# A new order of work in the mixer, and the final norm's third root placed sooner, in a hybrid attention and pooling layer

## The chip, the cores and the metric

The kernel runs on one core of one Trainium2 chip. A core has a matrix engine, TensorE (PE in the profile; PEld is its loading of stationary operands), and three others: VectorE (DVE), ScalarE (ACT) and GpSimd (POOL). SyncE (SP) only starts transfers. Each engine works through its own list in order and waits on semaphores for the others. Matmuls write to PSUM, eight banks of 128 x 512 float32; the other data lie in SBUF. The metric is the time of one execution in microseconds of device time, as the median of several.

## What is computed

One layer in float32: a half-weighted SwiGLU feed-forward block, a mixer, a second feed-forward block, and a norm of the rows. The sequence has 512 positions of 1024 channels.

```python
x = x + 0.5 * swiglu_ffn(rmsnorm(x, ffn1_norm), w_gate1, w_up1, w_down1)
x = x + hybrid_mixer(rmsnorm(x, mix_norm), w_in, ...)
x = x + 0.5 * swiglu_ffn(rmsnorm(x, ffn2_norm), w_gate2, w_up2, w_down2)
x = rmsnorm(x, final_norm)

def hybrid_mixer(h, ...):
    proj = h @ w_in                        # q, k, v, u, 512 channels each
    a = chunked_attention(q, k, v, ...)    # 8 heads of 64; q, k normed; bias; softmax
    p = multiscale_pool(u, ...)            # trailing means over 2, 4, 8, 16 minus the frame, then a 128 x 128 map
    return jnp.concatenate([a, p], axis=-1) @ w_out
```

A chunk of 64 positions attends to itself and the eight before it. With 512 positions that is every earlier chunk, so the scores are causal by blocks.

## The kernel before

All products are made from float32 values split in two parts, high (`whi`, `hhi`) and low (`wlo`, `hlo`): three matmuls (`mm3`, L176 to L178) stand for one product, a "unit" in what follows. ACT makes the high part and DVE subtracts it for the low part. The two feed-forward blocks use a product scheme with fewer multiplications, run by `ffn_up` and `Down`; the change does not touch their loops.

The mixer (from L894 on) works on tiles of 128 positions (t from 0 to 3). Its parts are Python generators:

- `project_qk` makes q and k of four heads (a half, 32 units, four PSUM banks of the tag `mm`); ACT empties each bank, scaled by the norm, into a row tile. `qk_norm` squares the rows (ACT), sums them per head (DVE, L1091), takes the reciprocal root on DVE (`rsqrt`), scales the four row tiles (DVE, L1122), has PE transpose them (L1130), and splits the result.
- `project_v` and `project_u` make v (32 units) and the four groups of pooled channels (8 units each). `pool` empties u on DVE (L1302), adds shifted copies on GpSimd (L1310: one addition for window 2, four for window 16), and finishes on DVE (L1317 to L1323); `pool_map` multiplies by the group's matrix.
- `scores` multiplies q by k for a pair of heads (L1201). Head dimension 64 fills half of PE's rows, so the two heads' matmuls go to the two halves by turns. Tile t has (t + 1) x 128 columns. `softmax` adds the bias, takes the row's minimum of the negated scores (DVE, L1170), exponentiates (ACT, L1176) and scales (ACT, L1182).
- `head` transposes the probabilities on PE (L1243) in three groups, splits them (L1222, L1225), multiplies by v (L1255) and splits the result (L1265 to L1270). Scores, transposes, head products and pool maps all take banks of the tag `a`, of which there are four.
- `project_out` makes the output projection (64 units) as its operands become ready, and `add` adds it to the residual and starts the next norm.

What stands where on PE, DVE, ACT and GpSimd is set by a planner, `run_parts` (L917). It keeps a model clock per engine; a part that has work gives its cost to `on`, and a part is taken when the time that it yields has come on PE's clock. Among parts that are ready the lowest rank is taken (`RANK_QK`, `RANK_HEAD`, `RANK_POOL`, `RANK_SCORES`, plus an entry of `RANKS`). `until` also holds a part back while an engine's model clock is over `SLACK` ahead of PE's. `products` is the background stream; `ORDER` sets it: before, first half of q and k, one group of u, second half, v, then three groups of u, then the output. The order thus planned is what the engines execute; the semaphores only say when.

```python
ORDER = (0, "u", 1, "v", "u", "u", "u")
RANK_QK, RANK_HEAD, RANK_POOL, RANK_SCORES = 1.5, 1.0, 1.035, 0.95
SLACK = 2.5
ACT_FIX, DVE_FIX, QK_NORM, NORM = 0.18, 0.08, 2.73, 3.5
```

The final norm is spread over the last product of the second feed-forward block. Rows are finished in tiles of 128; the third and fourth (t = 2, 3) come last. The last PSUM accumulations are p7: the third row's left half in one bank, the fourth row's in two banks of 256 columns. `residual` (L1475) adds a bank to the row, `settle` squares it with a sum over the row (ACT, L1488; DVE, L1483, for the very last part), `finish` takes the root on ACT (L1512), refines its reciprocal on DVE (`rsqrt_of`, L263 to L266), multiplies and stores (L1520, L1530).

Of the kernel before, what the change touches and what calls it, by code (L numbers as in the profile page):

```python
# [8 lines left out]
F32 = mybir.dt.float32  # L9
# [35 lines left out]
ORDER = (0, "u", 1, "v", "u", "u", "u")  # L45
RANK_QK, RANK_HEAD, RANK_POOL, RANK_SCORES = 1.5, 1.0, 1.035, 0.95
HOP = 0.1
SLACK = 2.5
ACT_FIX, DVE_FIX, QK_NORM, NORM = 0.18, 0.08, 2.73, 3.5
AHEAD, NORM_AT, FILL_AT, QK_ROOT = 2, 3, 7, ()  # L50
RANKS = {}

@with_exitstack
def layer(
# [202 lines left out]
    def rsqrt_of(v, root, out):  # L257

        n = v.shape[-1]
        y, a, b = (  # L260
            small.tile([P, n], F32, tag=f"rs{n}", name=name("rs"), bufs=3) for _ in range(3)
        )
        nc.vector.reciprocal(y, root)  # L263
        nc.vector.tensor_tensor(a, y, y, op=ALU.mult)
        nc.vector.scalar_tensor_tensor(b, a, -0.5, v, op0=ALU.mult, op1=ALU.mult)
        nc.vector.scalar_tensor_tensor(out, b, 1.5, y, op0=ALU.add, op1=ALU.mult)  # L266
# [627 lines left out]
    with tc.tile_pool(name="mix", bufs=1, reuse_waits="tile") as mpool:  # L894
# [51 lines left out]
        def t_mm3(n):  # L946
            return 3 * max(n / 2400, 0.107)
# [91 lines left out]

        qT, kT, aT, pT_out = [None] * 4, [None] * 4, [None] * 4, [None] * 4  # L1040
# [39 lines left out]
        def qk_norm(half, raw):  # L1080
# [38 lines left out]
            for t in range(NT):  # L1119
                yield from until(0.0, "dve")  # L1120
                q3 = raw[t][0].rearrange("p (h c) -> p h c", c=HD)
                nc.vector.tensor_tensor(  # L1122
                    q3, q3, rs[:, t, :].unsqueeze(2).to_broadcast([P, 8, HD]), op=ALU.mult
                )
                f = on("dve", t_dve(S))
            for j in (0, 2, 1, 3):
                yield from until(f)
                tp = yield from take("a")
                for t in range(NT):
                    nc.tensor.transpose(  # L1130
                        tp[:, t * P : (t + 1) * P], raw[t][0][:, j * P : (j + 1) * P], ident
                    )
                g = on("pe", 0.44)
                yield from until(g, "act", "dve")
                hi, lo = mtile(), mtile()
                split(tp, hi, lo, qk_sb[:, j // 2 : j // 2 + 1])
                g = on("dve", t_dve(S), on("act", t_act(S)))
                room["a"].append(g)
                (qT, kT)[j // 2][2 * half + j % 2] = (hi, lo), g
# [22 lines left out]
        def softmax(h, t, sc, f):  # L1162
# [8 lines left out]
                p, sc[:, :n], bias[h][0][:, S - n :], -1.0, BIG, op0=ALU.add, op1=ALU.min, accum_out=nm  # L1171
            )
            f = on("dve", t_dve(n))
            room["a"].append(f)
# [10 lines left out]
        def scores(pair):  # L1185
# [7 lines left out]
            for t in range(NT - 1, -1, -1):  # L1193
                n = (t + 1) * P
                sc = []
                for h in heads:
                    sc.append((yield from take("a")))
                for a, b in ((0, 0), (0, 1), (1, 0)):
                    for i in range(2):
                        rows = slice(i * HD, (i + 1) * HD)  # L1200
                        nc.tensor.matmul(  # L1201
                            sc[i][:, :n], qT[pair][0][a][rows, t * P : (t + 1) * P],
                            kT[pair][0][b][rows, :n], start=a + b == 0, stop=a == 1,
                        )
                f = on("pe", 2 * t_mm3(n))
                for i, h in enumerate(heads):
                    start(softmax(h, t, sc[i], f), RANK_HEAD + 0.01 * h, ("softmax", h))
                yield 0.0
            scored.update(heads)

        def head(h):
# [19 lines left out]
            for group in ((1, 3), (0,), (2,)):  # L1231
# [13 lines left out]
                start(evacuate(group, at, n, tp, on("pe", n / P * 0.11)), RANK_HEAD + 0.01 * h, ("turn", h))  # L1245
# [13 lines left out]
            f = on("pe", sum(t_mm3(n * P) for n in range(1, 5)) * 2 / 3)  # L1259
# [34 lines left out]
        def pool():  # L1294
            for g in (3, 2, 1, 0):
# [9 lines left out]
                s, step = u, 1  # L1305
                while step < win:
# [146 lines left out]
    with tc.tile_pool(name="act2", bufs=1, reuse_waits="tile") as apool:  # L1453
# [40 lines left out]
        def column(what):  # L1494
            return small.tile([P, 1], F32, tag="rc", name=name(what), bufs=6)
# [12 lines left out]
        def finish(t, v, part):  # L1508

            root, r = column("root"), column("r")  # L1510
            last = ssq[:, t, part : part + 1]
            nc.scalar.activation(root, last, AF.Sqrt, scale=1.0 / D, bias=v)  # L1512
            total = column("v")
            nc.vector.scalar_tensor_tensor(total, last, 1.0 / D, v, op0=ALU.mult, op1=ALU.add)
            rsqrt_of(total, root, r)
# [70 lines left out]
        with tc.manual_schedule(engines={E.PE, E.DVE, E.Activation}):  # L1586
            for tt in range(2):
                t = 2 + tt
                for i, at in enumerate(p7[tt]):
                    for g, a, w in late:  # L1590
                        down2.mms([[at]] * 2, g, a, w, (tt,), further=True)
                    residual(0, t, *at, scale=-0.5)
                    if i == 0 and tt:
                        settle(0, t, 0, *at[1:])
                        finish(t - 1, mean(t - 1, [1]), 0)
                        v = mean(t, [1, 0])
                    else:
                        settle(0, t, 2 * i, *at[1:])
            finish(t, v, 2)
# [81 lines left out]
```

## Time and profile before

| what | us |
|---|---|
| median of 3 runs (863.21 to 864.59) | 863.34 |
| the profiled execution | 864.34 |
| its span, from the first to the last instruction | 862.5 |
| busy in the span: PE | 846.9 |
| busy in the span: DVE | 715.1 |
| busy in the span: ACT | 501.4 |
| busy in the span: GpSimd | 120.5 |
| the mixer, some 354 to 527 us of the span | 173 |

In the profile L12 is line 12 of the kernel. A group of instructions is told as line, engine, operation, output<-inputs by the program's tile names, shape and count. A busy time counts an instruction from its start to its end; matmuls overlap, so that one of 512 columns lasts about 0.39 us while the next starts some 0.23 us after it. Where rows of a timeline have brackets, these hold the engine's idle time just before and who ended it. In a list of waits the columns are the total, how often, and the longest.

### The profile page before, as it was taken

How to read it: one execution, taken by the hardware profiler on the slowest of the kernel's cores; microseconds unless marked ns; L12 is line 12 of the kernel's file. 1: busy time of each engine (PE TensorE's matmuls, PEld its weight loads, DVE VectorE, ACT ScalarE, POOL GpSimd, SP SyncE). 2: the span in 40 equal slices, each digit the busy share in tenths (PEclk: the TensorE clock that was granted, in tenths of full speed). 3: DMA queues.
4: the chain of work that ended last, by engine and by line, in shares of the span. 5: the costliest groups of instructions: out<-in, count | busy, mean ns of one | idle time of the engine just before them, and what ended most of it. 6: DMA issues, size and time to landing. Idle time of an engine off the chain costs nothing.

```text
span 862.5 us, 14105 instructions
## 1 busy us (share of the span) xinstructions
PE 846.9 (98%) x5288; PEld 753.1 (87%) x5288; DVE 715.1 (83%) x1122; ACT 501.4 (58%) x859; POOL 120.5 (14%) x196
## 2 busy tenths in 40 slices
PE   9999999999999999989999999999999999999996
PEld 7889999999988888867878788889999999978885
DVE  7998889898897769685878667989988898787896
ACT  7445555555676556548647756355555555666573
POOL 0124322222000000120011000112121111122000
PEclk9999999999999999999999999999999999999999
DMA  8199998877576763322212026248778778899832
GB/s 291 55 279 258 302 267 200 201 214 167 150 235 205 251 210 135 102 86 84 75 56 92 25 73 230 89 146 228 216 227 208 191 200 222 251 317 351 256 107 98
DMA packets 72244, 158.50 MB, mean 184 GB/s; under 512 B 6112, under 2 KB 29168, under 8 KB 71792
## 3 DMA queue, kind: packets, MB, share of 16 engines
q1 hardware_dynamic: 49088, 110.93, 37.2%
q0 software_dynamic: 22656, 46.14, 24.8%
q8 instruction: 41, 0.67, 0.3%
q10 hardware_dynamic: 432, 0.54, 0.2%
q14 instruction: 27, 0.22, 0.1%
HBM read 153.38 MB, written 50.34 MB: 236 GB/s over the span
## 4 chain that ended last, share of the span: by engine, by line
PE 86%; DMA 6%; DVE 4%; ACT 2%; issue 1%; SPq 1%; ACTq 0%; DVEq 0%
PE mm L176 20%; PE mm L178 20%; PE mm L177 20%; PE a L176 7%; PE a L178 7%; PE a L177 7%; DMA raw<-in_wA_dram 4%; DMA raw<-in_wB_dram 1%; PE a L1201 1%; DVE wlo L478 1%; PE a L1255 1%; PE a L1243 1%; ACT whi L473 1%; DVE t L1122 1%; ACT prob L1182 1%
## 5 line engine op out<-in xcount | busy, mean ns | idle before, releaser
L131 ACT CAST whi<-raw 128x1024 fp32r<-128x1024 f32 (+2 forms) x115 | 107.4, 945 | 58.8 <-PE mm L177 17.4
L132 DVE TENSOR_TENSOR wlo<-raw,whi 128x1024 fp32r<-128x1024 f32 (+2 forms) x115 | 124.9, 1094 | 17.6 <-ACT whi L131 17.0
L176 PE MATMUL mm<-ha,whi 128*128 128x256 f32 x408 | 115.1, 282 | 0.0
L178 PE MATMUL mm<-ha,wlo 128*128 128x256 f32 x408 | 115.1, 282 | 0.0
L177 PE MATMUL mm<-ha,whi 128*128 128x256 f32 x408 | 114.6, 281 | 0.0
L569 ACT ACTIVATE t<-mm 128x256 f32<-128x256 f32 x102 | 39.1, 384 | 118.3 <-PE mm L178 117.5
L478 DVE TENSOR_TENSOR wlo<-wsum,whi 128x1024 fp32r<-128x1024 f32 x68 | 82.9, 1219 | 13.3 <-ACT whi L473 13.2
L177 PEld LDWEIGHTS mm<-ha,whi 128*128 128x128 f32 x408 | 77.4, 190 | 0.1
L176 PEld LDWEIGHTS mm<-ha,whi 128*128 128x128 f32 x408 | 77.2, 189 | 0.1
L178 PEld LDWEIGHTS mm<-ha,wlo 128*128 128x128 f32 x408 | 77.1, 189 | 0.0
L176 PE MATMUL mm<-hhi,whi 128*128 128x512 f32 x192 | 76.0, 398 | 0.3 <-ACT whi L131 0.3
L178 PE MATMUL mm<-hhi,wlo 128*128 128x512 f32 x192 | 75.0, 392 | 0.0
L177 PE MATMUL mm<-hlo,whi 128*128 128x512 f32 x192 | 74.8, 391 | 0.0
L706 POOL DMA_DIRECT2D wsum<-in_wB_dram x72 | 71.4, 1170 | 11.6 <-issue 8.2
L704 POOL COPY mark<-t 128x1 f32<-128x1 f32 x40 | 17.0, 425 | 379.3 <-DVE t L614 225.0
L473 ACT CAST whi<-wsum 128x1024 fp32r<-128x1024 f32 x68 | 67.8, 1045 | 3.1 <-PE mm L177 2.9
L177 PE MATMUL mm<-wlo,ah 128*128 128x512 f32 x176 | 68.8, 391 | 0.0
L178 PE MATMUL mm<-whi,ah 128*128 128x512 f32 x176 | 68.8, 391 | 0.0
L176 PE MATMUL mm<-whi,ah 128*128 128x512 f32 x176 | 68.6, 391 | 0.0
L478 DVE TENSOR_TENSOR wlo<-raw,whi 128x512 fp32r<-128x512 f32 x68 | 62.5, 951 | 5.5 <-ACT whi L473 3.4
L473 ACT CAST whi<-raw 128x512 fp32r<-128x512 f32 x68 | 56.3, 828 | 12.1 <-DMA raw<-in_wA_dram 12.0
L132 DVE TENSOR_TENSOR ah<-acts,ah 128x512 fp32r<-128x512 f32 (+1 forms) x72 | 45.7, 640 | 17.3 <-ACT ah L131 17.0
(224 smaller groups left out, 2380.1 us busy)
## 6 DMA issues: line engine op xcount, KB each, us to landing
raw<-in_wA_dram SPq DMA_DIRECT2D x87, 512.0 KB, 5.8
wsum<-in_wB_dram POOLq DMA_DIRECT2D x60, 512.0 KB, 7.5
raw<-wsum SPq DMA_DIRECT2D x40, 512.0 KB, 4.3
raw<-in_wB_dram SPq DMA_DIRECT2D x30, 512.0 KB, 4.8
wsum<-wsum POOLq DMA_DIRECT2D x20, 512.0 KB, 5.8
x<-in_xT_dram SPq DMA_DIRECT2D x16, 256.0 KB, 5.6
raw<-in_wQK_dram SPq DMA_DIRECT2D x8, 512.0 KB, 3.6
raw<-in_wO_dram SPq DMA_DIRECT2D x8, 512.0 KB, 3.4
```

Source lines behind the costliest of these rows:

```text
L131: nc.scalar.copy(hi, src)
L132: nc.vector.tensor_tensor(lo, src, hi.bitcast(F32), op=ALU.subtract)
L176: nc.tensor.matmul(acc, a[0], b[0], start=start, stop=False, **more)
L177: nc.tensor.matmul(acc, a[0], b[1], start=False, stop=False, **more)
L178: nc.tensor.matmul(acc, a[1], b[0], start=False, stop=stop, **more)
L473: nc.scalar.copy(hi, src)
L478: nc.vector.tensor_tensor(lo, src, hi.bitcast(F32), op=ALU.subtract)
L569: nc.scalar.activation(dst, src, AF.Copy, scale=scale)
L704: nc.gpsimd.tensor_copy(mark, after[:, 0:1])
L706: nc.gpsimd.dma_start(self.rows(i, g), self.rows(self.terms[i][at], g), **(dict(accum_op=ALU.add) if at else {}),)
L1122: nc.vector.tensor_tensor(q3, q3, rs[:, t, :].unsqueeze(2).to_broadcast([P, 8, HD]), op=ALU.mult)
L1182: nc.scalar.activation(p, p, AF.Copy, scale=rt)
```

## The change

The mixer's order is planned anew, and three pieces of code move.

- `ORDER` puts the second half of q and k directly behind the first; the first group of u follows it. Ranks, slack and the planner's costs are other numbers, `RANKS` gets entries, and the model cost of a unit is now 3 x (n / 2400 + 0.02) us.
- `scores` no longer goes tile by tile from 3 to 0, each in banks of its own. `GROUPS` says for each pair which tiles go together: a group is a list of bank sets, a bank set a list of tiles that lie side by side in one bank per head. For the first pair tiles 2 and 0 share a bank, then tiles 3 and 1 follow each other in two bank sets; for the other pairs tiles 1 and 0 share a bank. `softmax` gets its part of the bank, and the bank counts as free after its last tile.
- `pool` holds the planning of GpSimd's additions for a group back until a number of row tiles (`POOL_AFTER`) have been scaled by `qk_norm`.
- In the final norm the third row's root (`root_of`) is put on ACT right behind its square, ahead of the fourth row's square, and the reciprocal is refined in four DVE instructions in a row behind a halving, where it had five with the sum; the small tiles of `rsqrt_of` and of the columns get more buffers.

```diff
-ORDER = (0, "u", 1, "v", "u", "u", "u")
-RANK_QK, RANK_HEAD, RANK_POOL, RANK_SCORES = 1.5, 1.0, 1.035, 0.95
+ORDER = (0, 1, "u", "v", "u", "u", "u")
+RANK_QK, RANK_HEAD, RANK_POOL, RANK_SCORES = 1.66, 1.47, 0.935, 0.92
 HOP = 0.1
-SLACK = 2.5
+SLACK = 1.8
+POOL_AFTER = (8, 8, 7, 6)
+GROUPS = (
+    (((2, 0),), ((3,), (1,))),
+    (((1, 0),), ((2,),), ((3,),)),
+    (((3,),), ((2,),), ((1, 0),)),
+    (((1, 0),), ((2,),), ((3,),)),
+)
+STEP, SWITCH, TURN = 0.02, 0.32, 0.11
...
@@ scores @@
-            for t in range(NT - 1, -1, -1):
-                n = (t + 1) * P
+            for group in GROUPS[pair]:
                 sc = []
-                for h in heads:
-                    sc.append((yield from take("a")))
-                for a, b in ((0, 0), (0, 1), (1, 0)):
...
+                for _ in group:
+                    sc.append([])
+                    for h in heads:
+                        sc[-1].append((yield from take("a")))
+                on("pe", 2 * SWITCH)
+                for ts, banks in zip(group, sc):
+                    at = 0
+                    for t in ts:
+                        n = (t + 1) * P
+                        for a, b in ((0, 0), (0, 1), (1, 0)):
+                            for i in range(2):
+                                rows = slice(i * HD, (i + 1) * HD)
+                                nc.tensor.matmul(
+                                    banks[i][:, at : at + n],
+                                    qT[pair][0][a][rows, t * P : (t + 1) * P],
+                                    kT[pair][0][b][rows, :n], start=a + b == 0, stop=a == 1,
+                                    skip_group_check=True,
+                                )
+                        at += n
+                        f = on("pe", t_mm3(n))
...
@@ pool @@
+                while n_scaled[0] < POOL_AFTER[g]:
+                    yield None
                 while step < win:
...
@@ final norm @@
-        def finish(t, v, part):
+        def root_of(t, v, part):
+            root = column("root")
+            nc.scalar.activation(root, ssq[:, t, part : part + 1], AF.Sqrt, scale=1.0 / D, bias=v)
+            return root
+
+        def finish(t, v, part, root=None):
...
-            nc.scalar.activation(root, last, AF.Sqrt, scale=1.0 / D, bias=v)
-            total = column("v")
-            nc.vector.scalar_tensor_tensor(total, last, 1.0 / D, v, op0=ALU.mult, op1=ALU.add)
-            rsqrt_of(total, root, r)
+            nc.vector.tensor_scalar(half, v, -0.5, None, op0=ALU.mult)
+            nc.vector.scalar_tensor_tensor(
+                total, last, -0.5 / D, half, op0=ALU.mult, op1=ALU.add
+            )
+            nc.vector.reciprocal(y, root)
+            nc.vector.scalar_tensor_tensor(a, y, y, total, op0=ALU.mult, op1=ALU.mult)
+            nc.vector.scalar_tensor_tensor(r, a, 1.5, y, op0=ALU.add, op1=ALU.mult)
...
+            settle(0, first, 0, *p7[0][0][1:])
+            root = root_of(first, before, 0)
+            for i, at in enumerate(p7[1]):
+                for g, a, w in late:
+                    down2.mms([[at]] * 2, g, a, w, (1,), further=True)
+                residual(0, last, *at, scale=-0.5)
+                settle(0, last, 2 * i, *at[1:])
+                if i == 0:
+                    finish(first, before, 0, root)
+                    v = mean(last, [1, 0])
+            finish(last, v, 2)
```

On PE, DVE and ACT only the mixer and the final norm differ between the two programs; SP issues two loads and the bias rows in another order, and on GpSimd the bias tiles of heads 4 and 5 come ahead of the first pooled group's additions instead of behind.

72 lines of the change are left out of this document (37 added, 35 removed).

## Prediction

> **What bounds the kernel now.** I read the chain of waits first, by engine:
>
> ```profile
> PE 86%; DMA 6%; DVE 4%; ACT 2%; issue 1%; SPq 1%; ACTq 0%; DVEq 0%
> ```
>
> The end hangs on TensorE (PE) nearly all the way, so a new order can win only three things: time in which PE stands still, time it pays for changing between kinds of matmul, and the tail, where no matmul is left. Next I cut the span into stretches. The columns are the stretch, its length, then the busy time of PE, PE's weight loads, VectorE (DVE), ScalarE (ACT) and GpSimd (POOL), the granted clock and the DMA's share:
>
> ```profile
> 354.00:527.00 173.00, 168.64 (x864) 134.54 (x863) 122.31 (x281) 107.32 (x220) 16.55 (x26) 1.00 0.24 83
> 372.00:380.00 8.00, 5.39 (x24) 3.81 (x23) 7.14 (x9) 0.37 (x1) 5.40 (x4) 1.00 0.18 66
> 484.00:492.00 8.00, 6.38 (x42) 5.45 (x41) 3.95 (x9) 5.39 (x14) 0.00 (x0) 1.00 0.01 2
> 841.00:862.50 21.50, 13.77 (x89) 12.36 (x87) 13.86 (x42) 6.94 (x17) 0.00 (x0) 0.91 0.25 98
> ```
>
> The first row is the mixer: PE idles 173.00 - 168.64 = 4.36 us there. The next two rows hold nearly all of it: 8.00 - 5.39 = 2.61 us and 8.00 - 6.38 = 1.62 us. The last row is the final norm; there PE is without work for 21.50 - 13.77 = 7.7 us. The list of PE's waits (350 to 530 us; total, times, longest) names who was late:
>
> ```profile
> PE a L1130 <- DVE t L1122: 1.4, 2, 1.1
> PE mm L176 <- DVE u L1302: 1.2, 1, 1.2
> PE a L1243 <- DVE m L1270: 1.1, 1, 1.1
> PE a L1243 <- ACT prob L1182: 0.5, 1, 0.5
> ```
>
> The first two lie in 372:380: the transposes of q and k wait for DVE's scaled rows, and a projection waits for a PSUM bank that DVE empties into u. The other two lie in 484:492, at the transposes of heads 6 and 7. DVE's and GpSimd's timelines (start, length, line) tell why the scaled rows are late:
>
> ```profile
> 374.13 5.08 DVE L1122 TENSOR_TENSOR t<-t,z 128x512 f32<-128x512 f32 x4
> ...
> 415.75 2.49 DVE L1122 TENSOR_TENSOR t<-t,z 128x512 f32<-128x512 f32 x4
> ```
>
> ```profile
> 375.81 4.54 POOL L1310 TENSOR_TENSOR us<-us 128x525 f32<-128x525 f32 x3
> ```
>
> The same four scalings take 5.08 us while GpSimd sums and 2.49 us, with the other half of q and k, while it does not. So GpSimd's sums cost DVE 2.59 us there.
>
> **Term 1, the early stall.** Both halves of q and k are now projected before u. On DVE, in the mixer behind the first half's reciprocal root, stood before (t are the rows of q and k, z the root, u the pooled channels):
>
> ```order
> L995 TENSOR_TENSOR wlo_4302<-raw_4194,whi_4301 128x1024
> L1302 TENSOR_TENSOR u_4320<-mm_4242,rb_4202 128x512
> L1122 TENSOR_TENSOR t_4210<-t_4210,z_4294 128x512
> L1122 TENSOR_TENSOR t_4218<-t_4218,z_4294 128x512
> L1122 TENSOR_TENSOR t_4228<-t_4228,z_4294 128x512
> L1122 TENSOR_TENSOR t_4246<-t_4246,z_4294 128x512
> ```
>
> and stands now, at the same place:
>
> ```order
> L1009 TENSOR_TENSOR wlo_4306<-raw_4199,whi_4305 128x1024
> L1137 TENSOR_TENSOR t_4210<-t_4210,z_4289 128x512
> L1137 TENSOR_TENSOR t_4220<-t_4220,z_4289 128x512
> L1137 TENSOR_TENSOR t_4231<-t_4231,z_4289 128x512
> L1137 TENSOR_TENSOR t_4249<-t_4249,z_4289 128x512
> L1009 TENSOR_TENSOR wlo_4340<-raw_4243,whi_4339 128x1024
> ```
>
> The emptying of u, which released GpSimd's sums, is gone from in front of the scalings. Without the sums, rows that begin at 374.13 end at 374.13 + 2.49 = 376.6 and not at 374.13 + 5.08 = 379.2: 2.59 us sooner, and the missing u is worth about another 0.6. PE also has 17 units of three matmuls between the first half's projection and its transposes, where it had 15 (8 of u, 7 of the second half): two units more, 1.4 us at 0.23 us a matmul (the starts of two rows in the next term). That is some 4.6 us of room against 2.61 us of idle time: the whole 2.61 us goes, with 2 us to spare; if the cover failed, 2.61 us is what comes back.
>
> **Term 2, fewer changes to scores.** The scores use half of PE's rows, and each stretch of them pays at both edges. PE's timeline has two separate stretches (tiles of 256 and 128 columns) and the same two joined:
>
> ```profile
> 409.81 0.40 PE L178 MATMUL mm<-whi,hlo 128*128 128x512 f32 x1
> 410.13 0.62 PE L1201 MATMUL a<-m,m 64*128 64x256 f32 x6
> ...
> 412.26 0.55 PE L1201 MATMUL a<-m,m 64*128 64x128 f32 x6
> ...
> 413.08 0.39 PE L177 MATMUL mm<-wlo,hhi 128*128 128x512 f32 x1
> ```
>
> ```profile
> 475.08 0.39 PE L177 MATMUL mm<-m,whi 128*128 128x512 f32 x1
> 475.31 0.40 PE L178 MATMUL mm<-m,wlo 128*128 128x512 f32 x1
> 475.63 0.90 PE L1201 MATMUL a<-m,m 64*128 64x256 f32 x12
> ...
> 476.80 0.40 PE L177 MATMUL mm<-m,whi 128*128 128x512 f32 x1
> ```
>
> Ordinary matmuls start 0.23 us apart (475.31 - 475.08). From 409.81 to 413.08 are 3.27 us with eight of them (1.84 us): the two stretches cost 1.43 us. Joined: 476.80 - 475.31 = 1.49 us less two ordinary ones is 1.03 us. A join saves 0.40 us. On PE, in the scores of heads 0 and 1 (L1201 before, L1224 now; a are the score banks), stood before between two tiles a unit of projection:
>
> ```order
> L1201 MATMUL a_4425<-m_4374,m_4355 128x384
> L1201 MATMUL a_4439<-m_4374,m_4355 128x384
> L176 MATMUL mm_4316<-whi_4236,hhi_3926 128x512
> L177 MATMUL mm_4316<-wlo_4237,hhi_3926 128x512
> L178 MATMUL mm_4316<-whi_4236,hlo_3927 128x512
> L1201 MATMUL a_4446<-m_4374,m_4354 128x256
> L1201 MATMUL a_4451<-m_4374,m_4354 128x256
> ```
>
> and now one tile follows another, into the same two banks:
>
> ```order
> L1224 MATMUL a_4389<-m_4368,m_4357 128x384
> L1224 MATMUL a_4390<-m_4368,m_4357 128x384
> L1224 MATMUL a_4389<-m_4368,m_4356 128x128
> L1224 MATMUL a_4390<-m_4368,m_4356 128x128
> L1224 MATMUL a_4389<-m_4369,m_4356 128x128
> L1224 MATMUL a_4390<-m_4369,m_4356 128x128
> L1224 MATMUL a_4389<-m_4368,m_4357 128x128
> L1224 MATMUL a_4390<-m_4368,m_4357 128x128
> L190 MATMUL mm_4245<-whi_4239,hhi_3982 128x512
> ```
>
> Over the four pairs the order of before has 14 unbroken stretches (4, 4, 4 and 2), the new one 8 (two a pair, since where the plan has three groups two follow each other). Six joins at 0.40 us: -2.4 us. No row shows two tiles of scores in one bank. A join into a shared bank streams the same columns with the same weights, so it may save the whole 0.40; at worst it saves nothing. I take 0.40, the measured row being the nearest.
>
> **Term 3, the late stall.** On PE, at the first transposes of head 7 (prob), stood before, right behind the last two of head 6:
>
> ```order
> L1243 MATMUL a_5647<-ident,prob_5481 128x128
> L1243 MATMUL a_5647<-ident,prob_5468 128x128
> L1243 MATMUL a_5663<-ident,prob_5533 128x128
> L1243 MATMUL a_5663<-ident,prob_5486 128x128
> L1243 MATMUL a_5663<-ident,prob_5473 128x128 x2
> ```
>
> and now, with five units of the output projection, fifteen rows, between head 6 and these; the last two units are shown:
>
> ```order
> L190 MATMUL mm_5315<-m_5511,whi_5305 128x512
> L191 MATMUL mm_5315<-m_5512,whi_5305 128x512
> L192 MATMUL mm_5315<-m_5511,wlo_5307 128x512
> L1276 MATMUL a_5663<-ident,prob_5449 128x128
> L1276 MATMUL a_5663<-ident,prob_5468 128x128
> L1276 MATMUL a_5663<-ident,prob_5523 128x128 x2
> ```
>
> The fifteen rows are 15 x 0.23 = 3.45 us of cover, in which head 7's softmax and the emptied bank can arrive, against waits of 1.1 and 0.5 us. I take the 1.6 us as gone; at worst they stay.
>
> **Term 4, the final norm.** DVE, PE and ACT at the end:
>
> ```profile
> 853.01 0.42 DVE L1475 SCALAR_TENSOR_TENSOR xt<-a,xt 128x256 f32<-128x256 f32 x1 [1.11 <-PE a L178]
> ...
> 854.20 0.16 DVE L263 RECIPROCAL rs<-root 128x1 f32<-128x1 f32 x1 [0.43 <-ACT root L1512]
> ...
> 854.98 0.75 DVE L1520 SCALAR_TENSOR_TENSOR o<-xt,r,t 128x512 f32<-128x512 f32 x1
> ...
> 855.91 0.42 DVE L1475 SCALAR_TENSOR_TENSOR xt<-a,xt 128x256 f32<-128x256 f32 x1
> ...
> 857.35 0.16 DVE L264 TENSOR_TENSOR rs<-rs 128x1 f32<-128x1 f32 x1
> 857.55 0.16 DVE L265 SCALAR_TENSOR_TENSOR rs<-rs,v 128x1 f32<-128x1 f32 x1
> ```
>
> ```profile
> 854.49 0.28 PE L178 MATMUL a<-whi,ah 128*128 128x256 f32 x1
> ```
>
> ```profile
> 852.48 0.18 ACT L1488 ACTIVATION_READ_ACCUMULATOR t<-xt 128x1 f32 x1
> ...
> 853.88 0.28 ACT L1512 ACTIVATE root<-ssq,u 128x1 f32<-128x1 f32 x1
> ```
>
> The last matmul is over at 854.8, but DVE adds its result only at 855.91, since the third row's root and output stand in front. ACT could take that root at 852.7 and takes it at 853.88, behind a square of the fourth row. With the root first, DVE no longer waits 0.43 us for it: behind the sum that ends at 853.4 come five small steps, 0.2 us each where one needs the last, and the output begins at 854.2 to 854.4 instead of 854.98: 0.6 to 0.8 us. It also loses one small step of the last row's chain (857.55 - 857.35 = 0.20 us); the added halving hides under ACT's root. Sum -0.9 us, and all the rest of the tail, stores included, moves up by it.
>
> **Term 5, new waits.** The new order packs other places closer, and the page of before can't show them: v's fourth row now waits for the bank that u leaves. The nearest row is the 1.2 us wait of the same kind; below, no wait at all; above, as much again as all four waits of before, 4.2 us. I take 1.6, the one wait and a little.
>
> Sum: -2.6 - 2.4 - 1.6 - 0.9 + 1.6 = -5.9 us. The profiled execution took 864.34 us, its span 862.5 and 1.84 around it, and lies 1.00 us above the median of the three runs, 863.34; the sum comes off the median: **857.4 us**.
>
> **Rivals.** *Slower: softmax sets the pace.* Scores of a pair come in two bursts instead of four drops, and ACT has this to do in the mixer:
>
> ```profile
> L1176 ACT ACTIVATE prob<-prob,nm 128x512 f32<-128x512 f32 (+3 forms) x32 | 17.7, 555 | 9.0 <-DVE nm L1170 9.0
> L1182 ACT ACTIVATE prob<-prob,rt 128x512 f32<-128x512 f32 (+3 forms) x32 | 16.9, 558 | 0.1
> ```
>
> That is 34.6 / 4 = 8.65 us a pair. If PE stood 2.4 us at each pair's first transposes, 9.6 us in all, the gains of 7.5 would be eaten and the time 863.3 - 7.5 + 9.6 = 865.4; it decides from 1.9 us a pair on. Against it: ACT is busy 107.32 of 173.00 us, and a head's first transposes need one head's half, 4.3 us, while ten units (6.9 us) stand between pair 0's last scores and them. 0.08.
>
> *Gains handed on.* Each wait removed comes back a few units later, as the u bank's did in front of the scalings; 4.2 us of waits, half the joins' gain and the tail's 0.9 are lost: 863.3 - 7.5 + 4.2 + 1.2 + 0.9 = 862.1. 0.10.
>
> *GpSimd's sums are not behind.* No wait ties them to the scaled rows: the queue's first sum waits for u alone. If they met the second half's scalings, these would be 2.6 us late and PE with them: 857.4 + 2.6 = 860.0. Against it: u is emptied about 27 rows ahead of these scalings on DVE, root included. 0.10. The Trainium skill's page "SBUF — State Buffer" (how the doors into SBUF contend) says DVE and GpSimd hold one port pair by an exclusive lock against DVE instructions with two SBUF inputs. The pair 5.08 and 2.49 agrees; by that rule the sums also stop the root's small steps, which have two inputs too.
>
> *Readers kept off a shared bank.* If DVE may read the first tile of a bank only after the second tile is written, the first softmax starts later by that tile's six matmuls, 0.55 us in the row at 412.26; four shared stretches, all on the path: 857.4 + 2.2 = 859.6. For it: nothing in the order parts them. Against: DVE has other rows to do. 0.10. The Trainium skill's page "PSUM — Partial Sum Buffer" (section on bank collisions) asks for such a guard by bank, whatever the address; no run here shows a bank being read while written.
>
> **How the numbers follow.** My forecast has the remaining 0.62, its own range 855.2 (no new wait, and u's 0.6 on top) to 859. Faster by over 0.2%, which is what can be told from no change (1.7 us), holds in it and in the two rivals at 860: 0.82; the same 0.10; slower 0.08. The range runs from 855.2 to 861.6 and leaves out the last two cases.
>
> **What would show it.** Right: no PE wait on the scaled rows, both fours of scalings near 2.5 us, eight stretches of L1224, no PE wait over 0.5 us at the transposes of heads 6 and 7, the last xt under 0.5 us behind PE's last matmul. Wrong: PE idle in the mixer at 4 us or more; PE waits on prob at the first transposes of each pair would mean the slower rival.

## The result, and the profile after

The changed kernel takes 854.3 us (median of 4 runs, 853.65 to 855.89), the kernel before 863.78 (863.21 to 864.59) beside it: a ratio of 0.9892, 95% interval 0.9874 to 0.991. It is 9.5 us faster, where 5.9 were forecast, and lies under the range's lower end. The profiled execution took 854.88 us, its span 852.9. Lines have moved, the first ones by 14: `mm3` is now L190 to L192, scores L1224, the scaled rows L1137, the transposes of q and k L1146, those of the probabilities L1276, the product with v L1288.

The chain of waits by engine, after:

```profile
PE 93%; DMA 2%; DVE 2%; ACT 1%; issue 1%; SPq 0%; ACTq 0%; DVEq 0%
```

Busy time by stretch (columns as in the prediction), for the whole mixer, cut exactly: from the first product into a bank `mm` to the first transpose of x. The window 354 to 527 us, which stands for the mixer ahead of this, leaves out its first 14 us and takes in 7 us of the block behind it.

```profile
340.04:510.54 170.50, 170.50 (x886) 140.87 (x885) 129.38 (x299) 107.48 (x217) 16.49 (x30) 1.00 0.24 82
```

The same cut of the kernel before:

```profile
340.28:520.08 179.80, 175.48 (x887) 140.28 (x885) 131.06 (x299) 107.57 (x217) 18.03 (x30) 1.00 0.23 80
```

PE is busy in all of the mixer's 170.50 us, where it idled 179.80 - 175.48 = 4.32 us; the list of PE's waits between 335 and 515 us is empty. The mixer is 9.30 us shorter. The rest of the span's 862.5 - 852.9 = 9.6: 0.24 in front of the mixer, -0.69 in the second feed-forward block (its code is unchanged), and 0.73 in the tail (from the start of PE's last matmul to the end of the span):

```profile
844.16 0.42 DVE L1510 SCALAR_TENSOR_TENSOR xt<-a,xt 128x256 f32<-128x256 f32 x1 [1.10 <-PE a L192]
...
845.47 0.75 DVE L1564 SCALAR_TENSOR_TENSOR o<-xt,r,t 128x512 f32<-128x512 f32 x1
...
846.48 0.42 DVE L1510 SCALAR_TENSOR_TENSOR xt<-a,xt 128x256 f32<-128x256 f32 x1
```

DVE no longer waits for the third row's root: from the last addition to the third row to its output are 845.47 - 844.16 = 1.31 us, before 854.98 - 853.01 = 1.97. PE's last matmul starts at 845.64 and lasts 0.28, so the last xt stands 0.56 us behind its end (before 1.14, and under 0.5 forecast: this sign was missed narrowly).

### The profile page after: what moved, and what is told of

Read it like the earlier page. It is cut to its first block, busy times and chain, and to the rows that moved or that the text cites. A ratio compares the mean times of both kernels' runs of the same rounds, so it can differ in the third digit from the quotient of the medians.

```text
span 852.9 us, 14106 instructions
## 1 busy us (share of the span) xinstructions
PE 842.5 (99%) x5288; PEld 757.1 (89%) x5288; DVE 713.0 (84%) x1122; ACT 502.0 (59%) x859; POOL 117.5 (14%) x196
## 4 chain that ended last, share of the span: by engine, by line
PE 93%; DMA 2%; DVE 2%; ACT 1%; issue 1%; SPq 0%; ACTq 0%; DVEq 0%
PE mm L190 22%; PE mm L191 22%; PE mm L192 22%; PE a L191 7%; PE a L192 7%; PE a L190 7%; DMA raw<-in_wA_dram 2%; PE a L1288 1%; PE a L1224 1%; PE a L1276 1%; DVE wlo L492 1%; PE a L227 0%; PE a L1495 0%; DVE wlo L146 0%; PE a L1146 0%
## 5 line engine op out<-in xcount | busy, mean ns | idle before, releaser
L192 PE MATMUL mm<-ha,wlo 128*128 128x256 f32 x408 | 115.0, 282 | 0.0
L190 PE MATMUL mm<-ha,whi 128*128 128x256 f32 x408 | 114.9, 282 | 0.0
L192 PEld LDWEIGHTS mm<-ha,wlo 128*128 128x128 f32 x408 | 77.3, 189 | 0.0
L190 PEld LDWEIGHTS mm<-ha,whi 128*128 128x128 f32 x408 | 77.2, 189 | 0.1
L190 PE MATMUL mm<-hhi,whi 128*128 128x512 f32 x192 | 75.6, 396 | 0.0
L192 PE MATMUL mm<-hhi,wlo 128*128 128x512 f32 x192 | 74.7, 391 | 0.0
L192 PE MATMUL mm<-whi,ah 128*128 128x512 f32 x176 | 68.5, 389 | 0.0
L190 PE MATMUL mm<-whi,ah 128*128 128x512 f32 x176 | 68.4, 390 | 0.0
L718 POOL COPY mark<-t 128x1 f32<-128x1 f32 x40 | 14.1, 353 | 378.9 <-DVE t L628 229.6
```

The source lines that it names most:

```text
L190: nc.tensor.matmul(acc, a[0], b[0], start=start, stop=False, **more)
L192: nc.tensor.matmul(acc, a[1], b[0], start=False, stop=stop, **more)
L718: nc.gpsimd.tensor_copy(mark, after[:, 0:1])
```

## Experiments

All times of the mixer below are cut as above, from the one profiled execution of each kernel. They are the better measure of an edit in the mixer: where the mixer begins moved from 339.5 to 343.1 us between the profiles, and PE's waits ahead of it, in the first feed-forward block that no edit touches, from 2.1 us (middle_split) to 5.8 us (old_numbers). How well a mixer repeats can be seen in the new kernel and the four with dummy work in the first 96 matmuls: what stands behind these takes 145.14 to 145.19 us in all five. The kernel before ran again beside each; its medians were 863.18 to 864.31 us, and the ratios are to these.

| kernel | median us | ratio to before, 95% interval | mixer us |
|---|---|---|---|
| before | 863.78 | | 179.80 |
| new | 854.3 | 0.9892 (0.9874 to 0.991) | 170.50 |
| groups_only | 866.01 | 1.0025 (1.0012 to 1.0038) | 181.78 |
| order_only | 864.37 | 1.0004 (0.9992 to 1.0016) | 180.84 |
| old_numbers | 868.30 | 1.0044 (1.0029 to 1.0059) | 182.57 |
| no_table | 862.00 | 0.9988 (0.9968 to 1.0008) | 178.26 |
| unshared | 868.07 | 1.0039 (1.0022 to 1.0055) | 181.47 |
| pool_free | 856.68 | 0.9911 (0.9885 to 0.9938) | 172.42 |
| late_table_off | 855.52 | 0.9887 (0.9863 to 0.9911) | 171.37 |
| early_table_off | 863.57 | 0.9990 (0.9976 to 1.0005) | 178.47 |
| late_one_block | 856.04 | 0.9897 (0.9866 to 0.9929) | 171.80 |
| early_v_together | 858.45 | 0.9928 (0.9902 to 0.9954) | 174.36 |
| middle_split | 858.62 | 0.9937 (0.9911 to 0.9962) | 174.74 |
| brk8 | 858.11 | 0.9941 (0.9919 to 0.9962) | 174.22 |
| brk32 | 860.18 | 0.9951 (0.9935 to 0.9968) | 175.46 |
| sc8 | 862.42 | 0.9978 (0.9965 to 0.9991) | 177.78 |
| sc24 | 869.76 | 1.0057 (1.0039 to 1.0076) | 184.79 |

### What a break of the stream costs

Two pairs of kernels add the same dummy work to the new kernel, in few places or in many. Transposes first (`spare` is an idle bank; `n_units` counts the units of the first half of q and k):

```diff
+                    if spare is not None and n_units % 4 == 0 and n_units < 33:   # brk32: % 1, range(1)
+                        for j in range(4):
+                            nc.tensor.transpose(spare[:, j * P : (j + 1) * P], ident, ident)
```

brk8: 

> The new kernel with 32 extra transposes of the identity into an idle PSUM bank, put into the projection of the first half of q and k (the first 32 units of three matmuls), four together behind every fourth unit: 8 more breaks of the stream of ordinary matmuls. They add work that the layer does not need. Theory A (any break of the stream costs, transposes too, about 0.15 us): 32 x 0.11 + 8 x 0.15 = 4.7 us over the new kernel, 859.0. Theory B (only waits and changes to scores cost): 32 x 0.11 = 3.5, 857.8.

brk32: 

> The same 32 extra transposes, one behind each of the 32 units: 31 or 32 breaks, so 23 or 24 more than with four together, and the same work. Theory A: 23 x 0.15 = 3.5 us over the variant with four together, 862.5. Theory B: within 0.5 us of it.

PE's timeline in brk8 and in brk32 (the dummies are L1080):

```profile
346.58 0.39 PE L192 MATMUL mm<-whi,hlo 128*128 128x512 f32 x1
346.81 0.60 PE L1080 MATMUL a<-ident 128*128 128x128 f32 x4
347.16 0.48 PE L190 MATMUL mm<-whi,hhi 128*128 128x512 f32 x1
347.48 0.40 PE L191 MATMUL mm<-wlo,hhi 128*128 128x512 f32 x1
```

```profile
346.97 0.39 PE L192 MATMUL mm<-whi,hlo 128*128 128x512 f32 x1
347.20 0.27 PE L1080 MATMUL a<-ident 128*128 128x128 f32 x1
347.23 0.48 PE L190 MATMUL mm<-whi,hhi 128*128 128x512 f32 x1
347.54 0.39 PE L191 MATMUL mm<-wlo,hhi 128*128 128x512 f32 x1
```

The matmul behind a break starts its successor 0.32 us later and not 0.23, which looks like a price of 0.09; but the first transpose gives it back: alone it holds PE 347.23 - 347.20 = 0.03 us, in a row of four 0.35 / 4 = 0.09. From the start of the matmul in front to that of the second one behind, less two ordinary ones, four transposes in one break take 347.48 - 346.58 - 0.46 = 0.44 us, 0.11 each, and one alone takes 347.54 - 346.97 - 0.46 = 0.11. So the break itself costs nothing that these rows show. Counted over more of them: from the first matmul of the fifth unit to the first of the second half, with the same other instructions between, are 23.81 us in brk8 (7 breaks, 28 transposes) and 23.93 in brk32 (28 breaks, 28 transposes), 0.12 us for 21 breaks, **under 0.01 us a break**.

The mixers differ by more, 175.46 - 174.22 = 1.24 us, but 1.14 of it lies in the first four units, where brk32 places the last transposes of the first feed-forward block (L879) sooner and PE waits for their operand. PE's timeline there in brk8 and in brk32:

```profile
344.34 1.47 PE L879 MATMUL a<-ident,acts 128*128 128x128 f32 x12
```

```profile
343.83 1.58 PE L879 MATMUL a<-ident,acts 128*128 128x128 f32 x12 [0.52 <-DVE acts L814]
```

Theory A, 0.15 a break, falls; theory B, that only waits and changes to scores cost, holds.

Dummies of the scores' shape:

```diff
+                    if spare is not None and n_units < 33:
+                        for j in range(6 if n_units % 4 in (2,) else 0):   # sc24: 2 if ... in (1, 2, 3)
+                            rows = slice(j % 2 * HD, (j % 2 + 1) * HD)
+                            nc.tensor.matmul(
+                                spare[j % 2][:, : 2 * P],
+                                cut(n2.h[k], t * P, P)[0][rows, :],
+                                cut(n2.h[k], 0, 2 * P)[0][rows, :], start=True, stop=True,
+                                skip_group_check=True,
+                            )
```

sc8: 

> The new kernel with 48 extra matmuls of the scores' shape (64 rows, 256 columns, both row halves in turn, into two idle PSUM banks), put into the projection of the first half of q and k in 8 stretches of six, each between two units of three ordinary matmuls. The layer does not need them. A stretch of six of this shape cost 1.43 us for two with the smaller one of 128 columns, so some 0.75 each: the mixer 8 x 0.75 = 6 us longer than the new kernel's 170.5, 860 to 861.

sc24: 

> The same 48 extra matmuls in 24 stretches of two: 16 more stretches, the same work. If a stretch of scores costs 0.40 us at its edges, as the joined and separate stretches of the kernel before had it: 16 x 0.40 = 6.4 us over the variant with stretches of six. If the edges cost what a break by transposes cost (1.24 us for 23, 0.05 each): 0.9 us.

PE's timeline in sc8 and in sc24:

```profile
350.97 0.39 PE L192 MATMUL mm<-whi,hlo 128*128 128x512 f32 x1
351.29 0.62 PE L1081 MATMUL a<-hhi 64*128 64x256 f32 x6
351.83 0.50 PE L190 MATMUL mm<-whi,hhi 128*128 128x512 f32 x1
352.17 0.40 PE L191 MATMUL mm<-wlo,hhi 128*128 128x512 f32 x1
```

```profile
350.89 0.40 PE L192 MATMUL mm<-whi,hlo 128*128 128x512 f32 x1
351.22 0.38 PE L1081 MATMUL a<-hhi 64*128 64x256 f32 x2
351.53 0.50 PE L190 MATMUL mm<-whi,hhi 128*128 128x512 f32 x1
351.87 0.40 PE L191 MATMUL mm<-wlo,hhi 128*128 128x512 f32 x1
```

Six take 351.83 - 351.29 = 0.54 us, two take 0.31, and both pay 0.1 us ahead (351.29 - 350.97 = 0.32 for 0.23) and 0.1 behind (352.17 - 351.83 = 0.34). Whole, a stretch of six costs 352.17 - 350.97 - 0.46 = 0.74 us and one of two 351.87 - 350.89 - 0.46 = 0.52, so two stretches more for the same six matmuls cost 3 x 0.52 - 0.74 = 0.82. Over the same matmuls as with the transposes, sc8 takes 26.11 us (7 stretches) and sc24 31.65 (21), with 42 dummies in each: 5.54 us for 14, **0.40 us a stretch**, as expected.

The mixers differ by 184.79 - 177.78 = 7.01 us for 16, which would be 0.44 each, but the wait at L879 is in it again (0.54 us of idle time in sc24, none in sc8). Of the 7.28 us that sc8 took where 6 were expected, 0.9 lie in these first units too (6.29 us against the new kernel's 4.63, with one stretch of 0.74). A stretch in the half-row shape is worth joining; a break by transposes is not worth avoiding.

### One part of the change at a time

groups_only and old_numbers are built from the new code, with the kernel before's planner numbers and final norm; order_only from the kernel before.

```diff
 # order_only: the kernel before with
-ORDER = (0, "u", 1, "v", "u", "u", "u")
+ORDER = (0, 1, "u", "v", "u", "u", "u")
 # groups_only: GROUPS as in the change, everything else as before
 # old_numbers: GROUPS and ORDER as in the change, everything else as before
```

groups_only: 

> The kernel before with the new grouping of score tiles alone: the old order of projections, the old planner numbers, GpSimd's sums not held back, the old final norm. On PE the order then has 11 stretches of scores where the kernel before has 14, and 42 streams of ordinary matmuls where it has 50. Theory A: three joins at 0.40 and five other breaks less at 0.15 are 2.0 us: 861.8; theory B: 3 x 0.40 = 1.2: 862.6. Either way the early stall (PE waiting for the scaled rows and for the bank of u) stands as before. If tiles in one bank kept readers off, it would be 863.8 or more.

order_only: 

> The kernel before with the new order of projections alone (both halves of q and k ahead of u); nothing else of the change. On PE it has 45 streams of ordinary matmuls (before 50), 13 stretches of scores (14), 12 of probability transposes (15). Theory A: the early stall, 2.6 us by the profile's idle time and 2.9 by the pitch of the starts, and five breaks at 0.15 with 0.25 more for the score stretch, 1.0: 859.9 to 860.2. Theory B: 2.6 + 0.4 = 3.0: 860.8. If the wait is only handed on to a later place: 863 and a PE wait of 1 us or more somewhere in the mixer. If GpSimd's sums meet the second half's scalings when nothing holds them back: PE waits 2 us or more there, 862 or more.

old_numbers: 

> The new order of projections and the new grouping with every planner number of the kernel before (ranks, slack, costs, no table, GpSimd's sums not held back) and the old final norm. 10 stretches of scores, 38 streams. Theory C: two stretches 0.8, the tail 0.75, waits of 2 to 5 us: 858 to 861. Theory D: 854.3 + 0.8 + 0.75 = 855.9, no PE wait over 0.5 us.

All three expected gains that did not come: groups_only is slower than before by 0.25%, order_only cannot be told from it, and both parts together are slower still. In groups_only the early stall stands as before (2.6 us of waits), and the list of waits behind it has 3.8 us where the kernel before has 1.6, most of it at transposes of probabilities. That eats the gain of the joins; whether readers that wait for a whole shared bank have part in it was not tried. PE's waits in order_only's mixer say why it gains nothing:

```profile
PE a L1243 <- ACT prob L1182: 1.7, 2, 1.2
PE a L176 <- ACT m L134: 1.5, 1, 1.5
PE a L176 <- DVE m L1270: 1.1, 1, 1.1
```

The early stall is gone, as the theory had it, and 4.3 us of waits stand at two pool maps and at the last heads' transposes instead. They bring a second loss. Behind the waits at 484 to 488 us the granted clock, the share of full speed at which PE may run, falls to half for 3.4 us, and ordinary matmuls start 0.43 us apart. In this stretch its mean is 0.57:

```profile
488.00:492.00 4.00, 4.00 (x15) 3.27 (x15) 2.77 (x5) 1.50 (x4) 0.00 (x0) 0.57 0.01 4
```

By that pitch it costs some 3.4 x (1 - 0.23 / 0.43) = 1.6 us. The same fall, 3.4 us long, stands in old_numbers (from 489.5 us) and in unshared (from 490.2 us), behind waits of 3.5 and of 2.4 and 2.0 us, and in no other mixer of the table. It isn't of the profiled executions alone: over whole executions the mean granted clock of these three kernels was 0.990 to 0.998, that of the kernel before 0.997 to 0.999. When it falls is not settled by these runs: no_table waits 1.3 and 1.8 us between 480 and 487 us and keeps the full clock. In old_numbers one product with v alone waits 3.5 us:

```profile
488.45 0.50 PE L1282 MATMUL a<-pT,v 128*128 128x512 f32 x1 [3.51 <-ACT pT L1249]
```

Next the new kernel without its table, without the grouping, and without the holding back of GpSimd:

```diff
 # no_table
+RANKS = {}
 # unshared
+GROUPS = ((((3,),), ((2,),), ((1,),), ((0,),)),) * 4
 # pool_free
-POOL_AFTER = (8, 8, 7, 6)
+POOL_AFTER = (0, 0, 0, 0)
```

no_table: 

> The new kernel with its table of ranks by part emptied (RANKS = {}); the order of projections, the grouping, the other numbers and the final norm stay. On PE it has 10 stretches of scores (new 8) and 40 streams of ordinary matmuls (38). Theory C (each part alone only hands its waits on; it is the table that puts the pieces where nothing waits): two stretches, 0.8, and waits of 1.5 to 4 us in the mixer: 856.6 to 859, with PE waits shown behind ACT or DVE at the probability transposes. Theory D (the new order and groups free PE by themselves): 854.3 + 0.8 = 855.1 and no PE wait over 0.5 us.

unshared: 

> The new kernel with every tile of scores in banks of its own and in a group of its own, largest first as before: on PE 13 stretches of scores (new 8), 14 of probability transposes (12), 44 streams (38). Joins alone: 5 x 0.42 = 2.1, and two breaks by transposes at 0.05: 856.5, no PE wait over 0.5 us. If the numbers fit the new groups only (Theory C): waits of 1.5 us or more come on top, 858 or more.

pool_free: 

> The new kernel with GpSimd's sums not held back in the plan (POOL_AFTER all 0). DVE's order then has the mean of the first group (which waits for GpSimd) in front of the second half's scaled rows, and the sums may run beside them. If holding them back matters: the second four scalings take up to 5 us instead of 2.5, PE waits 1 to 2.6 us at the q and k transposes, 855.3 to 857. If putting both halves of q and k ahead of u was enough: 854.3 within 0.5 us and no PE wait there.

PE's waits in the mixer of no_table, and in that of unshared:

```profile
PE a L1270 <- DVE m L1297: 1.8, 1, 1.8
PE a L1282 <- DVE pT L1252: 1.3, 1, 1.3
PE mm L184 <- DVE u L1329: 1.1, 1, 1.1
```

```profile
PE a L1271 <- ACT prob L1194: 2.4, 1, 2.4
PE a L1271 <- DVE m L1298: 2.0, 1, 2.0
PE a L1219 <- DVE nm L1181: 1.3, 2, 1.1
```

Theory C holds, and by more than it said: the table alone is worth 7.8 us of mixer. Unshared is 11 us longer than the new kernel, with 5 x 0.40 = 2.0 us of stretches, 5.7 us of waits in the list and 1.6 of the halved clock. The numbers fit one set of groups only; so what unshared measures is not the worth of a join.

Pool_free is 1.9 us longer, for neither reason that was written down. GpSimd's and DVE's timelines there:

```profile
403.20 3.60 POOL L1345 TENSOR_TENSOR us<-us 128x525 f32<-128x525 f32 x3
```

```profile
411.69 1.89 DVE L1137 TENSOR_TENSOR t<-t,z 128x512 f32<-128x512 f32 x3
```

The sums run at 402 to 407 (the first of the four from 402.06), where the new kernel has them too (402.23), and the scalings begin at 411.69: they don't meet, held back or not. What changed is the plan behind them: at 480 us PE's output projection waits 1.4 us for a head's result (0.45 and 0.95, at its two parts).

### Which piece of the table keeps which wait away

```diff
 RANKS = {
-    ("head", 0): 0.05, ("head", 2): 3, ("head", 3): -0.02, ("head", 4): -1,
-    ("head", 6): -10, ("pool", 0): -10, ("qk", 0): -0.05, ("scores", 3): -1,
-    ("softmax", 0): -10, ("softmax", 2): 0.5, ("softmax", 3): 0.5, ("softmax", 6): -0.5,
-    ("turn", 1): 0.5, ("turn", 2): 0.02, ("turn", 5): -0.05, ("turn", 6): 3,
-    ("turn", 7): -10,
 # late_table_off leaves out head 4 and 6, scores 3, softmax 6, turn 5 to 7
 # early_table_off leaves out the other ten
 # late_one_block leaves out pool 0 alone; middle_split head 2 alone
 # early_v_together keeps what late_table_off leaves out, and head 2
 }
```

late_table_off: 

> The new kernel with the table's entries for heads 4 to 7 and the last scores taken out; those for heads 0 to 3 stay. 8 stretches of scores, 38 streams, as in the new kernel. Emptying the whole table made the mixer 7.8 us longer, 4.7 of it in gaps of PE at heads 6 and 7. If these entries keep the last heads from waiting: the mixer is 3 to 6 us over 170.5, with the gaps at the last heads' transposes and products with v. If the table's worth comes from the early entries: under 1 us.

early_table_off: 

> The new kernel with the table's entries for heads 0 to 3, for q and k and for the pooled groups taken out; those for heads 4 to 7 stay. 10 stretches of scores and 41 streams (new 8 and 38): 2 x 0.42 and three breaks at 0.05 are 1.0 us in any case. If the early entries keep the u bank's wait and the first heads' waits away: 1.0 + 1.3 + 1.3 = 3.6 us over the mixer's 170.5, gaps at 399 and 447 us as with the emptied table. If the waits at the last heads come back too, since those are what is left when an early piece shifts: 5 us or more.

late_one_block: 

> The new kernel without the table's entry for the last pooled group. PE's order is the new one up to the scores of the last pair; behind them the transposes of heads 6 and 7 stand next to each other again (14 in a row, as in the kernel before), where the new kernel has five units of the output projection between. 8 stretches of scores, 38 streams, as in the new kernel. If those five units are what covers head 7's softmax and bank: the mixer is 1.6 (the idle time of before there) to 3.4 us (the gaps of the kernel with the emptied table) over 170.5, in gaps inside that block. If the wait was gone for another reason: under 0.5.

early_v_together: 

> The same late order as late_one_block, and in addition the early entries out, except that for head 2: the eight first units of v stand together (v's fourth row right behind the first three), where the new kernel has head 0's ten transposes between the third and the fourth. 9 stretches of scores (8), 39 streams (38). If these transposes cover the bank that u leaves: over late_one_block 1.3 for that wait, 0.6 for the second gap at 408 us and 0.5 for the stretch and the breaks: 2.4 us. If the bank is free in time anyway: 0.5.

middle_split: 

> The new kernel without the table's entry for head 2: the order is the new one up to the products of head 1 with v; behind them the scores of the third and fourth pair fall into 10 stretches (8) and 41 streams (38). Edges alone: 2 x 0.44 + 3 x 0.05 = 1.0 us, no gap over 0.5. If the late heads wait again because the units that covered them are used up sooner: 3 us or more.

Late_table_off took its cheaper branch: 0.9 us, not 3 to 6. Early_table_off took its dearer one, 8.0 us, with waits at the u bank and at the last heads. (The expectations read some gaps of PE too large: at heads 6 and 7 in no_table the pauses are 1.4 and 2.0 us by the starts, not 4.7, and there is none at 447 us.) Late_one_block then has one wait alone. PE's timeline there, and at the same place in the new kernel:

```profile
478.51 1.26 PE L1272 MATMUL a<-ident,prob 128*128 128x128 f32 x10
480.88 0.63 PE L1272 MATMUL a<-ident,prob 128*128 128x128 f32 x4 [1.11 <-DVE m L1299]
```

```profile
476.47 1.25 PE L1276 MATMUL a<-ident,prob 128*128 128x128 f32 x10
477.48 0.48 PE L190 MATMUL mm<-m,whi 128*128 128x512 f32 x1
...
481.01 0.60 PE L1276 MATMUL a<-ident,prob 128*128 128x128 f32 x4
```

Five units of the output projection, 481.01 - 477.48 = 3.5 us, stand between the two blocks in the new kernel and cover a bank that DVE empties late. Without them the mixer is 171.80 - 170.50 = 1.30 us longer. The profile shows 1.11 of idle time for that: rows of PE overlap, and the idle time counts from the end of the matmul in front, not from where the next one could have started.

Early_v_together adds 2.56 us to that (expected 2.4). PE's timeline at v's fourth row in it:

```profile
400.26 0.40 PE L188 MATMUL mm<-whi,hlo 128*128 128x512 f32 x1
401.79 0.51 PE L186 MATMUL mm<-whi,hhi 128*128 128x512 f32 x1 [1.13 <-DVE u L1331]
...
402.69 0.90 PE L1220 MATMUL a<-m,m 64*128 64x256 f32 x12
```

And the new kernel's PE there, with DVE's row for the bank:

```profile
397.78 0.39 PE L192 MATMUL mm<-hhi,wlo 128*128 128x512 f32 x1
398.10 1.47 PE L1224 MATMUL a<-m,m 64*128 64x256 f32 x18
399.50 0.50 PE L190 MATMUL mm<-whi,hhi 128*128 128x512 f32 x1
...
401.76 0.97 PE L1224 MATMUL a<-m,m 64*128 64x512 f32 x6
402.66 0.50 PE L190 MATMUL mm<-whi,hhi 128*128 128x512 f32 x1
```

```profile
401.40 0.68 DVE L1335 TENSOR_TENSOR u<-mm,rb 128x512 f32<-128x512 f32 x1
```

In both kernels DVE empties u late, behind the splitting of a weight. In the new one the scores of heads 2 and 3 (1.40 + 0.90 us) stand between u's last product (397.78) and v's fourth row (402.66), and the bank is free at 402.08, 0.6 us in time. In the other, these scores come behind. So the expectation named the wrong cover (head 0's transposes, which stand inside u's products) and the right wait: 1.3 us by the starts (401.79 - 400.26 - 0.23). One more stretch is 0.40 of the rest; 0.9 us stays unexplained. Middle_split, with two stretches more (0.8 us), came out 4.2 us longer, with 2.5 us of PE waits at heads' transposes and the output projection, as its second branch had it.

No kernel of these has a shorter mixer than the new one; by its whole time late_table_off can't be told from it (0.9887 against 0.9892).

## Why the prediction was wrong

The direction was right and the size too small: 5.0 us were forecast for the mixer (2.6 + 2.4 + 1.6 - 1.6) and 0.9 for the tail, 9.3 and 0.73 came.

**Term 5 is the step that failed.** It charged 1.6 us for new waits, of which none came, and named one: v's fourth row waiting for the bank that u leaves. The wait is real and costs 1.1 to 1.3 us (no_table, early_table_off and early_v_together all have it), but not in the new order, where scores cover it. The same holds at the end. The step took the new order as the old one packed closer and charged it by waits of before. The table of ranks had settled precisely that, and it could have been asked of the order: what stands on PE between the emptying of u and v's fourth row.

**Terms 1 and 3, mechanism right, size too small.** They were read as idle time, 2.61 and 1.62 us. PE's timeline of the kernel before has the early ones once more:

```profile
372.68 0.39 PE L178 MATMUL mm<-whi,hlo 128*128 128x512 f32 x1
374.26 0.50 PE L176 MATMUL mm<-whi,hhi 128*128 128x512 f32 x1 [1.20 <-DVE u L1302]
...
377.14 0.38 PE L1130 MATMUL a<-ident,t 128*128 128x128 f32 x2
377.80 0.33 PE L1130 MATMUL a<-ident,t 128*128 128x128 f32 x1 [0.28 <-DVE t L1122]
379.26 0.33 PE L1130 MATMUL a<-ident,t 128*128 128x128 f32 x1 [1.13 <-DVE t L1122]
```

From start to start, less 0.23 us for the matmul and 0.11 for a transpose, the pauses are 1.35 us at the bank of u and 0.45 + 1.35 at the transposes: 3.15. The late ones are 0.55 at the first block and 1.28 at the second, and late_one_block, where the second came back alone, is 1.30 longer: 1.8 together. That is 5.0 us and not 4.2. One more pause, of 0.24 us in the output projection (460.52 - 459.97, less the 0.31 that is usual behind transposes), is too short for the list of waits; the new mixer has none like it. The signs came: both fours of scalings take 2.49 us, there are eight stretches of L1224, and no PE wait is left at heads 6 and 7. But that order_only frees PE from the early stall and gains nothing shows what term 1 alone is worth. The removal counts only because every later place was also covered.

The sums' price itself held: in groups_only, which keeps the old order, the four scalings take 5.08 us again beside GpSimd, and 2.49 in the new kernel, where the sums run at another time.

```profile
376.26 5.08 DVE L1131 TENSOR_TENSOR t<-t,z 128x512 f32<-128x512 f32 x4
```

```profile
410.96 2.49 DVE L1137 TENSOR_TENSOR t<-t,z 128x512 f32<-128x512 f32 x4
```

The Trainium skill's page "SBUF — State Buffer" (section "Who interferes with whom") has a DVE instruction with two SBUF inputs and a GpSimd instruction that reads SBUF lock each other out of a shared port pair; both pairs of numbers agree with it.

**Term 2, right in place and in size.** 14 stretches became 8, the forecast's count, and sc8 and sc24 give 0.40 us for one, the forecast's price: 2.4 us. That tiles in one bank give the whole 0.40 was not tried apart.

The sum by these prices is 3.15 + 1.8 + 0.24 + 2.4 = 7.6 of 9.30 us. Between pauses, ordinary matmuls also start a little closer, 0.2279 us against 0.2301 (means over 542 and 519 starts): 1.1 us, which no term had. All kernels with the new planner numbers have the short pitch (0.2279 to 0.2286), no_table and unshared among them, and the four with the old numbers the long one (0.2296 to 0.2301); why was not tried. Some 0.6 us stays open.

So of the 4.3 us that the mixer gained beyond the forecast, 1.6 are the waits of term 5 that did not come, 0.8 the pauses of terms 1 and 3 that were read too short, 0.24 the pause that was not in the list, 1.1 the pitch, and the rest is open.

**Term 4.** 0.73 of 0.9: the third row's output came 0.66 us sooner, inside the 0.6 to 0.8. The last row's chain, from its last addition to its output, lost 0.12 us (before 857.93 - 855.91 = 2.02, now 848.37 - 846.48 = 1.89) where 0.20 were forecast.

**The rivals.** None set the time. *Softmax sets the pace*: PE waits for no probabilities. *GpSimd's sums are not behind*: pool_free shows that they end 4.9 us ahead of the scalings even when nothing holds them. *Readers kept off a shared bank*: they are kept off, but it costs nothing on the path. In the second pair the matmuls of the bank's first tile end at 398.72 us and those of its second at 399.00, and DVE begins on the first tile only behind both:

```profile
399.14 0.43 DVE L1186 CUSTOM_DVE_ANT_0 prob<-a,bias 128x256 f32<-128x256 f32 x1 [0.44 <-PE a L1224]
```

In the fourth pair it is the same (463.27, 463.54, and DVE at 463.58); in the other two DVE was busy with other rows. No PE wait follows. This agrees with the guard by bank that the Trainium skill's page "PSUM — Partial Sum Buffer" (section on bank collisions) asks for; no run shows what happens without it. *Gains handed on* is wrong for the whole change and right for its two parts in the mixer, order_only and groups_only: at 0.10 it was the rival to take most seriously, and what parted it from the forecast was the table.

## What to carry to other kernels

A wait removed from a full pipeline moves on unless every later place has cover; so ask of a new order, for each wait that it could bring, what stands between the releasing and the waiting instruction, and charge nothing where that is longer than the release is late. Try the parts of such a change together with the numbers that were fitted to them: alone, both parts here gained nothing, together with the old numbers they lost, and with the new numbers but no table they came out even (0.9988). Read pauses of PE from start to start against the steady pitch; the idle column is smaller, here 4.2 against 5.0 us. And before a price is taken from the difference of two kernels, look where in the trace the difference lies: 1.1 of the 1.24 us between brk8 and brk32 was a wait that had nothing to do with the breaks.

## What the runs showed of the hardware

- A stretch of half-row matmuls between ordinary ones costs 0.40 us at its edges, whether it has two matmuls or six (sc8 and sc24: 5.54 us for 14).
- A break by transposes between ordinary matmuls costs under 0.01 us beyond its transposes (brk8 and brk32: 0.12 us for 21): the matmul behind it is 0.09 late, but its first transpose holds PE for 0.03 only.
- The idle time that the profile shows before a matmul is some 0.2 us less than the pause costs: 1.11 against 1.30, and 1.13 against 1.30.
- In three kernels (order_only, old_numbers, unshared) the granted clock fell to half for 3.4 us behind waits of PE between 484 and 490 us; in order_only ordinary matmuls then started 0.43 us apart instead of 0.23.
